# Two pairs of heads in step in a fused FNet and RWKV-7 block

## The chip, the cores and the metric

The program runs on one core of a Trainium2 chip. The metric is the device time of one execution, in microseconds (us), as the median over several runs. PE is TensorE, DVE VectorE, ACT ScalarE, POOL GpSimd; SP issues the DMAs of this kernel, all on one queue that is worked in order.

## The reference

```python
proj = x @ w_in                                   # 256 tokens, 2048 -> 512 + 3*1536 + 480 columns
y_fourier = real(fft2(proj[:512] in 4 groups))
p = p + (0.5*(prev + next) - p) * mu_shift        # centred shift of the other columns
r, k, v = ...                                     # 24 heads of 64, i.e. 12 pairs of heads
w_f, w_b = decay(tanh(low rank) @ w_up)           # low rank of 64, both directions
a_f, a_b = sigmoid(a0 + low rank @ a_up)
def step(state, r, w, k, v, a, b):                # along the tokens, forward and backward
    sa = state @ a
    state = state * w + outer(sa, b) + outer(v, k)
    return state, state @ r
y = group_norm(y_forward + y_backward); y = (y + bonus(r, k, r_k) * v) * (sigmoid(p_g) @ g_up)
h = layernorm(ALPHA*x + concat(y_fourier, y) @ w_out)
out = layernorm(ALPHA*h + (silu(h @ w_gate) * (h @ w_up)) @ w_down)     # 2048 -> 5632 -> 2048
```

All inputs are float32.

## The kernel before, in words

**Products.** A float32 weight tile is split in two: ACT casts it to float32r (`hi`), DVE subtracts that from the raw tile (`lo`), and the product is hi*hi + hi*lo + lo*hi. `weights()` loads one half tile of 512 KB into one of three `raw` buffers and splits it into two hi/lo pairs of 128x512, from rings of eight. A projection of 256 tokens onto 128 columns (`project`, `summed`) is 48 matmuls of 128x256 from two half tiles. Small products have plain float32 operands.

**The mixer** works on one pair of heads (128 columns) after the other, twelve in all. `prepare` computes K and R, the decays (low-rank products, exponentials), the normalised key and the scores `w` of each chunk of 64 tokens. The recurrence is chunked: four chunks a direction, and in each a 64x64 unit triangular matrix is inverted. `invert` does this in two parts. The 32x32 diagonal blocks are solved by substitution on POOL: 31 steps of two operations (`tmp` = product, `tt` = sum), on rows that DVE has laid out (`wt`, `wx`) and that DMAs take to DRAM (`md`) and back as a broadcast (`mt`). After the last step DVE transposes `tt` into `to`, and 32x32 matmuls on PE merge the blocks (`v1`, `xo`, into `ti`). `values` projects V into `sv`; `recur` walks the four chunks: `g` (scores times values) on PE, `gs` a copy by ACT, `u` = `ti` times `gs` on PE, copies into `sv`, `s` (the new state) on PE, and the outputs into the bank `yb`. A group norm (`bst`, `mv`, `rs`, `yn`) ends the pair, and its 128 rows go to DRAM as `mix`.

**The output projection** (`tokens_out` with `w_out`) takes `mix` back in, and runs over 32 half tiles of weights: four quarters of columns (q) by eight pairs of 128 rows, in an order by hand: of q 0 and 1 first the rows of `ORDER[:-1]`, then those of the last, then q 2 and 3. Its last `keep` tiles do their first 128 tokens before their other 128, so that the norm of the first half starts earlier; `keep` is half of the hi/lo pairs on hand (ring and `spare`). Then come the first norm, the gated feed-forward (176 half tiles) and the down projection (88, by `tokens_out` too, with eight further pairs as `spare`).

**What sets the order.** Nothing is issued as it is written. Operations are recorded with their dependences (`Program.add`), and `schedule` lists them with costs and latencies by hand, per engine; the best of 49 settings of two weights is issued. On PE it prefers, for a time, the array shape (rows by columns of the array that a matmul occupies) in use; `fused()` records several matmuls as one operation that nothing splits. Each engine works its list in order. Nearly all instructions carry the line of the loop that issues them (L307 before, L316 after), so rows are told apart by tile names.

Of the kernel before, what the change touches and what calls it, by code (L numbers as in the profile page):

```python
# [48 lines left out]
NV = V_LB + 12  # L49
# [18 lines left out]
class Program:  # L68
# [35 lines left out]
    def region(ap):  # L104

        dims, t = [list(d) for d in ap.ap], ap.tensor
        if "PSUM" in str(t._space):
            if not t.name.startswith("ch"):
                return 15, 15
            first = ap.offset % 512  # L110
            last = first + sum(s * (n - 1) for s, n in dims[1:])
            return 15, sum(1 << q for q in range(first // 128, last // 128 + 1))
        if "SB" not in str(t._space):
            return 1, 1
# [25 lines left out]
    def cost(self, eng, method, outs, ins, k, args):  # L140
# [3 lines left out]
        kw_op = k.get("op")  # L144
        if eng == "pe":
# [6 lines left out]
            return max(m, n) * 4 / 2.4 * side + 3 if m != 32 else 30  # L152
        if eng == "act":
            return 54 + 0.833 * n + 93 * ptrs + (40 if not psum else 0)
        if eng == "pool":
            if kw_op == OP.pow:
                return 500
            return (40 if method == "memset" else 147) + (0.9 if method == "memset" else 2.15) * n + 150 * ptrs
        if eng == "sp":
            return max(500, 4 * self.count(outs[0]) * list(outs[0].ap)[0][1] / 360)  # L160
# [3 lines left out]
        return 69 + (0.52 if half else 1.04) * n + 60 * ptrs  # L164
# [6 lines left out]
    def add(self, queue, method, args, kw):  # L171
# [27 lines left out]
        banks = {x.tensor.name for x in outs + ins if "PSUM" in str(getattr(x.tensor, "_space", ""))}  # L199
# [29 lines left out]
    def schedule(self, weight, hold):  # L229
# [14 lines left out]
        while left:  # L244
# [27 lines left out]
            if k is not None and k != kind[e]:  # L272
                kind[e] = k
                if e == 3:
                    t += 87
                    since = t
                else:
                    c += 1300
# [47 lines left out]
ORDER = (2, 3, 4, 5, 6, 0, 1, 7)  # L326
FOURIER = 0
# [4 lines left out]
def body(ctx, tc, i, out):  # L332
# [15 lines left out]
    ch.tiles = [t[:, c:c + 256] for c in (0, 256) for t in chain[2:]]  # L348
    nar = Ring(psum, "nar", [128, 512], 0)
    nar.tiles = [t[:, c:c + 128] for c in range(0, 512, 128) for t in chain[0:2]]  # L350
# [3 lines left out]
    def weights(src, spare=[]):  # L354
# [3 lines left out]
        for j in range(2):  # L358
# [3 lines left out]
            dve.tensor_tensor(lo, half, hi.bitcast(F32), op=OP.subtract)  # L362
# [26 lines left out]
    ws = Ring(consts, "w", [128, 2, 2, 4, 128], 3)  # L389
# [28 lines left out]
    hmu = consts.tile([128, 44], F32, name="hmu")  # L418
    omm = consts.tile([128, 44], F32, name="omm")
    dve.tensor_scalar(hmu, vec[:, V_MU:V_MU + 44], 0.5, None, op0=OP.mult)  # L420
    dve.tensor_scalar(omm, vec[:, V_MU:V_MU + 44], -1.0, 1.0, op0=OP.mult, op1=OP.add)
    hw0 = consts.tile([128, 48], F32, name="hw0")
    dve.tensor_scalar(hw0, vec[:, V_W0F:V_W0F + 48], 0.5, None, op0=OP.mult)
    hka = consts.tile([128, 12], F32, name="hka")
    omka = consts.tile([128, 12], F32, name="omka")
    dve.tensor_scalar(hka, vec[:, V_KA:V_KA + 12], 0.5, None, op0=OP.mult)
    dve.tensor_scalar(omka, vec[:, V_KA:V_KA + 12], -0.5, 1.0, op0=OP.mult, op1=OP.add)
    mhalf = consts.tile([128, 4], F32, name="mhalf")
    dve.memset(mhalf, -0.5)

    def project(wsrc, tl, src):
# [4 lines left out]
        for h in range(2):  # L436
            summed(acc, weights(wsrc[tl, h]), 8 * h, src)
# [6 lines left out]
    pps = ring("pp", [128, S + 2], 2)  # L444
    pss = ring("ps", [128, S], 1)
# [7 lines left out]
    def shifted(tl, dst):  # L453
        acc = project(i["w_in"], tl, xT)
        p, s = pps.next(), pss.next()
        act.activation(p[:, 1:S + 1], acc, AF.Copy, scale=hmu[:, tl:tl + 1])
        dve.tensor_tensor(s, p[:, 0:S], p[:, 2:S + 2], op=OP.add)
        dve.scalar_tensor_tensor(dst, acc, omm[:, tl:tl + 1], s, op0=OP.mult, op1=OP.add)


    lora = mx.tile([128, 2, S], F32, name="lora")
    low = mx.tile([128, 2, 2, S], F32R, name="low")
    for j, tl in enumerate((T_W, T_A)):
        t = lora[:, j, :]
# [3 lines left out]
        for d in range(2):  # L468
            (a0, a1), (b0, b1) = HEAD[d], HEAD[1 - d]
            act.copy(low[a0:a1, d, j, :], t[a0:a1])  # L470
            dve.tensor_tensor(low[b0:b1, d, j, :], t[a0:a1], low[a0:a1, d, j, :].bitcast(F32), op=OP.subtract)
    for j, tl in enumerate((T_G0, T_G1)):
# [9 lines left out]
    rmask = const("rmask", [128, 260])  # L482
    eye4 = const("eye4", [128, 8, 32])
    R = {n[0]: ring(*n) for n in (
        ("up", [128, 4, 128], 1), ("uh", [128, 4, 128], 1, F32R), ("ul", [128, 4, 128], 1, F32R),
        ("upg", [128, 2, 128], 1), ("k", [128, S], 1), ("th", [128, 2, S], 1), ("ta", [128, 2, S], 1),
        ("e", [128, 2, 4, 65], 1), ("f", [128, 2, 4, 65], 1), ("dec", [128, 4, 2], 3),
        ("kx", [128, S], 1), ("sq", [128, S], 1), ("kk", [128, S], 1), ("r", [128, S], 1),
        ("bs", [128, S], 2), ("xb", [128, 2, 4, 3, 64], 1), ("ar", [128, 2, 4, 3, 64], 3), ("bg", [128, 2 * S], 1),
        ("bk", [128, 2, 8, 64], 3), ("v", [128, S], 3), ("sv", [128, 4, 2, 2, 64], 2), ("wt", [128, 256], 1),  # L490
# [309 lines left out]
    for p in range(NPAIR):  # L800
        st = prepare(p)
        if p == FOURIER:
            fourier_in()
# [259 lines left out]
```

## Time and profile before

| | us |
|---|---|
| median of three runs (1424.67 to 1429.63) | 1426.9 |
| profiled execution, its own time | 1424.8 |
| its span, first to last instruction | 1422.9 |
| PE busy, share of the span | 1340.8, 94% |
| DVE, ACT, POOL busy | 954.1, 789.9, 501.5 |
| mean granted clock of TensorE | 0.974 of 2.4 GHz |

The mixer fills the first 610 us, the output projection lies across its end up to about 660 us, the feed-forward and the down projection fill the rest. Busy shares are means over these stages, so each stage has to be read by itself.

### The profile page before, as it was taken

Reading aid. Unit: us, or ns where it says so; the run is one execution under the profiler, and the core shown is the slowest. Engines: PE = TensorE matmul, PEld = TensorE weight load, DVE = VectorE, ACT = ScalarE, POOL = GpSimd, SP = SyncE. Lnnn points to the kernel's source line nnn. Section 1 sums busy time; section 2 is a strip of 40 time slices with the busy share of each in tenths; the row PEclk is TensorE's granted clock in tenths of the full one; section 3 lists DMA queues with packets and bytes.
Section 4 is the critical chain, followed back from the end, with each engine's and each line's share of the span. In section 5 each row is a group of like instructions: output and inputs, shape, how many; then the busy total and the mean of one; then the engine's idle time right before and its main releaser. Section 6 shows DMA issues by size and latency. Waiting matters only on the chain.

```text
span 1422.9 us, 26852 instructions
## 1 busy us (share of the span) xinstructions
PE 1340.8 (94%) x9828; PEld 1173.3 (82%) x9828; DVE 954.1 (67%) x1803; ACT 789.9 (56%) x1670; POOL 501.5 (35%) x1032
## 2 busy tenths in 40 slices
PE   8988999888889989998999999999999999999996
PEld 7987888878888876777888888888888888888886
DVE  6758778887888786668565556555555555555555
ACT  6556665666666665544555555555555554444441
POOL 1165878778888887102211111111111110000002
PEclk9999999999999998999999999999999999999998
DMA  8543332333333335463565555555555555656552
GB/s 277 189 152 119 105 112 94 109 103 103 116 116 101 105 125 175 156 202 127 195 237 181 192 187 185 191 186 185 191 184 188 192 181 195 194 195 195 194 196 102
DMA packets 73164, 232.32 MB, mean 163 GB/s; under 512 B 8136, under 2 KB 17224, under 8 KB 72392
## 3 DMA queue, kind: packets, MB, share of 16 engines
q1 hardware_dynamic: 73032, 230.61, 49.8%
q8 instruction: 77, 1.26, 0.4%
q14 instruction: 55, 0.45, 0.1%
HBM read 224.28 MB, written 6.29 MB: 162 GB/s over the span
## 4 chain that ended last, share of the span: by engine, by line
PE 63%; POOL 22%; DVE 7%; issue 4%; ACT 2%; DMA 1%; DVEq 0%; SPq 0%; POOLq 0%; ACTq 0%
PE ch L307 23%; PE mm L307 19%; PE sc L307 14%; POOL tmp L307 9%; POOL tt L307 9%; PE yb L307 7%; DVE lo L307 1%; POOL rs L307 1%; DVE w L307 1%; DVE f L307 1%; DVE ti L307 1%; ACT hi L307 1%; DVE yn L307 1%; POOL xb L307 1%; DMA mt<-md 1%
## 5 line engine op out<-in xcount | busy, mean ns | idle before, releaser
L307 DVE TENSOR_TENSOR lo<-raw,hi 128x512 fp32r<-128x512 f32 x758 | 555.5, 741 | 356.2 <-ACT hi L307 350.2
L307 ACT CAST hi<-raw 128x512 fp32r<-128x512 f32 x758 | 465.0, 620 | 411.0 <-PE mm L307 120.9
L307 PE MATMUL mm<-xT,hi 128*128 128x256 f32 (+1 forms) x1776 | 419.5, 320 | 6.7 <-ACT hi L307 5.6
L307 PEld LDWEIGHTS mm<-xT,hi 128*128 128x128 f32 x1776 | 301.8, 198 | 24.6 <-ACT hi L307 5.8
L307 PE MATMUL mm<-xT,lo 128*128 128x256 f32 (+1 forms) x1072 | 304.1, 292 | 0.0
L307 PEld LDWEIGHTS mm<-xT,lo 128*128 128x128 f32 x1072 | 209.9, 197 | 5.3 <-DVE lo L307 0.4
L307 PE MATMUL ch<-xT,hi 128*128 128x512 f32 x528 | 186.0, 399 | 0.0
L307 POOL TENSOR_TENSOR fe<-fe,fe 128x256 f32<-128x256 f32 x44 | 32.8, 747 | 406.0 <-DVE fe L307 385.6
L307 POOL TENSOR_TENSOR tmp<-mt,tt 128x60 f32<-128x60 f32 (+24 forms) x372 | 151.8, 408 | 52.5 <-DMA mt<-md 27.1
L307 POOL TENSOR_TENSOR tt<-tt,tmp 128x60 f32<-128x60 f32 (+24 forms) x372 | 141.8, 381 | 25.4
L307 PE MATMUL ch<-xT,lo 128*128 128x256 f32 x528 | 142.7, 281 | 0.0
L307 PE MATMUL sc<-xT,hi 128*128 128x512 f32 x352 | 121.9, 397 | 0.0
L307 PEld LDWEIGHTS ch<-xT,hi 128*128 128x128 f32 x528 | 97.2, 189 | 19.5
L307 PEld LDWEIGHTS ch<-xT,lo 128*128 128x128 f32 x528 | 99.8, 189 | 4.6
L307 POOL TENSOR_TENSOR lrs<-lrs,mhalf 128x1 f32<-128x1 f32 x4 | 3.9, 973 | 281.4 <-DVE lrs L307 281.4
L307 PE MATMUL sc<-xT,lo 128*128 128x256 f32 x352 | 93.3, 280 | 0.0
L307 PE MATMUL ch<-hi,h 128*128 128x512 f32 x264 | 88.4, 389 | 0.0
L307 PEld LDWEIGHTS sc<-xT,hi 128*128 128x128 f32 x352 | 63.8, 188 | 13.1
L307 PE MATMUL mm<-hi,h 128*128 128x512 f32 (+1 forms) x248 | 72.9, 358 | 0.0
L307 PEld LDWEIGHTS sc<-xT,lo 128*128 128x128 f32 x352 | 66.4, 189 | 2.9
L307 PE MATMUL yb<-xT,hi 128*128 128x512 f32 x176 | 63.7, 396 | 0.0
L307 PEld LDWEIGHTS ch<-hi,h 128*128 128x128 f32 x264 | 49.6, 188 | 10.4
(221 smaller groups left out, 2213.2 us busy)
## 6 DMA issues: line engine op xcount, KB each, us to landing
raw<-in_w_gu_dram SPq DMA_DIRECT2D x176, 512.0 KB, 3.8
raw<-in_w_down_dram SPq DMA_DIRECT2D x88, 512.0 KB, 4.2
raw<-in_w_in_dram SPq DMA_DIRECT2D x84, 512.0 KB, 3.5
raw<-in_w_out_dram SPq DMA_DIRECT2D x32, 512.0 KB, 3.6
mt<-md SPq DMA_DIRECT2D x12, 512.0 KB, 4.3
up<-in_lora_up_dram SPq DMA_DIRECT2D x12, 256.0 KB, 4.2
raw<-in_xT_dram SPq DMA_DIRECT2D x8, 256.0 KB, 4.7
raw<-in_w_in_dram SPq DMA_DIRECT2D x8, 256.0 KB
```

The lines of the kernel that those rows point to most:

```text
L307: getattr(o["q"].engine, method)(*args, **kw)
```

## The change

- **Two pairs in step.** The loop takes two pairs of heads at a time (`P`, six rounds), and the recurrence of round P-1 is written after the preparation of round P. `recur` does both pairs in each of its steps: one copy or state update serves both, each kind of product is one `fused` run of 64-row matmuls, and half-bank tiles of PSUM (`nar`) hold both pairs.
- **Substitution on 16x16 blocks.** `extract` computes the transposed score blocks on PE (eight 64x64 products a pair), masks them, and takes 16x4x16 pieces to DRAM, 16 DMAs a pair. `substitute` does 15 steps for both pairs at once, writes `tt` to DRAM (`ms`) and reads it back in 16 pieces as blocks of a 32x32 matrix (`eb`, and transposed `et`). `invert` merges 16 to 32 and 32 to 64 with 224 32x32 matmuls for two pairs, in runs that go round the four 32-row quadrants.
- **Low-rank products** are four plain float32 matmuls with 64 rows instead of eight in float32r, and the split of `up` into `uh`, `ul` goes.
- **Weights of the mixer:** POOL instead of DVE computes `lo` of the second half of each `w_in` tile (`shared`). The hi/lo rings have six buffers instead of eight.
- **Buffers:** `ch` has whole banks, `w`, `ar`, `bk`, `v` four buffers, `sv` and `ti` one for both pairs; `bonus` and gate products move to DVE.
- **Output projection:** `ORDER` and the order of tiles follow the pairs as they come ready; the Fourier projection moves from the first pair to the third. `spare` is empty, so `keep` is 3 instead of 5 here and 7 instead of 8 in the down projection.
- **Costs of the planner** are changed, among them those of POOL, of small DMAs, of partial partitions, and of a switch of the array shape.

```diff
-ORDER = (2, 3, 4, 5, 6, 0, 1, 7)
...
+ORDER = (2, 3, 4, 5, 0, 1, 6, 7)
...
     raws = Ring(consts, "raw", [128, 1024], 3)
-    his = Ring(consts, "hi", [128, 512], 8, F32R)
-    los = Ring(consts, "lo", [128, 512], 8, F32R)
+    his = Ring(consts, "hi", [128, 512], 6, F32R)
+    los = Ring(consts, "lo", [128, 512], 6, F32R)
...
-    def weights(src, spare=[]):
+    def weights(src, spare=[], shared=False):
...
-            dve.tensor_tensor(lo, half, hi.bitcast(F32), op=OP.subtract)
+            (pool if shared and j else dve).tensor_tensor(lo, half, hi.bitcast(F32), op=OP.subtract)
...
-            summed(acc, weights(wsrc[tl, h]), 8 * h, src)
+            summed(acc, weights(wsrc[tl, h], shared=True), 8 * h, src)
...
         th, ta = R["th"].next(), R["ta"].next()
...
-            js = slice(2 * d, 2 * d + 2)
-            dve.tensor_tensor(ul[a0:a1, js, :], up[a0:a1, js, :], uh[a0:a1, js, :].bitcast(F32), op=OP.subtract)
-        for d in range(2):
-            z = sc.next()
+        zs = sc.next(), sc.next()
+        with pr.fused():
             for j in range(2):
-                for u in (uh, ul):
-                    pe.matmul(z[:, j * S:(j + 1) * S], u[:, 2 * d + j, :], low[:, d, j, :], start=u is uh, stop=u is ul)
+                for d, (a0, a1) in enumerate(HEAD):
+                    pe.matmul(zs[d][:, j * S:(j + 1) * S], up[a0:a1, 2 * d + j, :], lora[a0:a1, 2 + j, :], start=True, stop=True)
+        for d, z in enumerate(zs):
...
+    def extract(p, st, mt):
...
+        tp, m0 = sc.next()[:, 0:S], R["sq"].next().rearrange("p (c s) -> p c s", s=64)
+        with pr.fused():
+            for c in range(4):
+                for h, (a0, a1) in enumerate(HEAD):
+                    pe.matmul(tp[a0:a1, c * 64:(c + 1) * 64], ar[a0:a1, 0, c, 0, :], xb[a0:a1, 0, c, 0, :], start=True, stop=True)
+        dve.tensor_tensor(m0, tp.rearrange("p (c s) -> p c s", s=64), tmask[:, None, :].to_broadcast([128, 4, 64]), op=OP.mult)
...
+            for d in (0, 1):
+                for n, (h, b, a) in enumerate(quads):
+                    for k in range(2):
+                        q, r, cs = n * 16 + k * 8 + 4 * d, slice(a + 16 * k, a + 16 * k + 16), slice(32 * b + 16 * k, 32 * b + 16 * k + 16)
+                        sp.dma_start(out=mdp[q:q + 4].rearrange("c (x y) -> x c y", y=16), in_=w[r, 1, h, :, cs] if d else m0[r, :, cs])
+            sp.dma_start(out=mt[:, p % 2].rearrange("p x y -> p (x y)"), in_=mdp[:, None].to_broadcast([64, 2, 256]))
...
+    def substitute(P, mt):
+        msp = ms[P % 2]
+        tt, tmp, e, et = (R[n].next() for n in ("tt", "tmp", "eb", "et"))
+        act.copy(tt, eye2[:, None].to_broadcast([128, 2, 8, 16]))
+        for s in range(15):
+            m, t = min(8, s + 1), 15 - s
+            x = tmp[:, 0:2 * m * t].rearrange("p (n j t) -> p n j t", n=2, t=t)
+            pool.tensor_tensor(x, mt[:, :, None, s + 1:16, s].to_broadcast([128, 2, m, t]),
+                               tt[:, :, 0:m, s:s + 1].to_broadcast([128, 2, m, t]), op=OP.mult)
+            pool.tensor_tensor(tt[:, :, 0:m, s + 1:16], tt[:, :, 0:m, s + 1:16], x, op=OP.add)
+        with pr.ahead(AHEAD):
+            sp.dma_start(out=msp.rearrange("(n p) x -> p n x", n=2), in_=tt.rearrange("p n m t -> p n (m t)"))
+            for j in range(2):
+                for n, (h, b, a) in enumerate(quads):
+                    for k in range(2):
+                        r = a + 16 * k
+                        sp.dma_start(out=e[r:r + 16, 8 * j:8 * j + 8, 16 * k:16 * k + 16],
+                                     in_=msp[j * 128 + r:j * 128 + r + 16].rearrange("(c u) (m t) -> (u m) c t", u=2, t=16))
+        dve.transpose(et.rearrange("p c t -> p (c t)"), e.rearrange("p c t -> p (c t)"))
+        return (e, et), (et, e)
...
+        with pr.fused():
+            for q in range(16):
+                j, d, c = q // 8, q // 4 % 2, q % 4
+                for h, b, a in quads:
+                    pe.matmul(vp[a:a + 32, q * 32:(q + 1) * 32], ws[j][a:a + 32, d, h, c, 32 * b:32 * b + 32],
+                              diag[d][1][a:a + 32, q, :], start=True, stop=True)
+        dve.copy_predicated(z.rearrange("p (n q) t -> p n (q t)", n=2),
+                            zmask.bitcast(mybir.dt.uint32)[:, None, :].to_broadcast([128, 2, 256]),
...
             u = nar.next()
-            for d in range(2):
-                pe.matmul(u[:, d * 64:d * 64 + 64], ti[:, d * 4 + cd[d], :], gs[:, d * 64:d * 64 + 64], start=True, stop=True)
+            with pr.fused():
+                for n, d, h, a0, a1 in jobs:
+                    o = n * 128 + d * 64
+                    pe.matmul(u[a0:a1, o:o + 64], ti[a0:a1, n * 8 + d * 4 + cd[d], :], gs[a0:a1, n, d, :], start=True, stop=True)
...
-    for p in range(NPAIR):
-        st = prepare(p)
-        if p == FOURIER:
-            fourier_in()
-        invert(p, st)
-        tokens(st)
-        values(p, st)
-        recur(p, st)
+    last = None
+    for P in range(NPAIR // 2 + 1):
+        if P < NPAIR // 2:
+            dec, mt = R["dec"].next(), R["mt"].next()
+            sts = []
+            for n in range(2):
+                sts.append(prepare(2 * P + n, dec[:, n]))
+                if P == 1 and n == 0:
+                    fourier_in()
+                extract(2 * P + n, sts[n], mt)
+                tokens(sts[n])
+                sts[n]["v"] = R["v"].next()
+                shifted(T_V + 2 * P + n, sts[n]["v"])
+            diag = substitute(P, mt)
+        if P:
+            recur(P - 1, *last)
+        if P < NPAIR // 2:
+            sv = R["sv"].next()
+            for n in range(2):
+                values(2 * P + n, sts[n], sv)
+            last = sts, invert(sts, diag), sv, dec
...
...
```

The order of POOL's instructions before, late in the mixer, within the substitution of one pair (`tmp`, `tt`); `bs` and `e` are of `prepare`:

```order
L307 TENSOR_TENSOR tmp_152<-mt_150,tt_151 128x54
L307 TENSOR_TENSOR bs_133<-th_121 128x256
L307 TENSOR_TENSOR tt_151<-tt_151,tmp_152 128x2x27
L307 MEMSET e_123 128x4 x2
L307 TENSOR_TENSOR tmp_152<-mt_150,tt_151 128x52
L307 TENSOR_TENSOR tt_151<-tt_151,tmp_152 128x2x26
```

The same engine after, in the last steps of the substitution of a round of two pairs:

```order
L316 TENSOR_TENSOR bs_124<-th_117 128x256
L316 TENSOR_TENSOR tmp_143<-mt_141,tt_142 128x48
L316 TENSOR_TENSOR lo_75<-raw_66,hi_69 128x512
L316 TENSOR_TENSOR tt_142<-tt_142,tmp_143 128x16x3
L316 TENSOR_TENSOR tmp_143<-mt_141,tt_142 128x32
L316 TENSOR_TENSOR tt_142<-tt_142,tmp_143 128x16x2
L316 TENSOR_TENSOR lo_77<-raw_67,hi_71 128x512
L316 TENSOR_TENSOR tmp_143<-mt_141,tt_142 128x16
L316 TENSOR_TENSOR lo_79<-raw_65,hi_73 128x512
```

One operation now serves two pairs, and the splitting of weights (`lo`) stands between the steps. On the SP queue, before, in the mixer (`raw` are the weights, `md` and `mt` the way through DRAM, `mix` a pair's result):

```order
L307 DMA raw_67<-in_w_in_dram 128x1024
L307 DMA md_182<-wx_148 128x256
L307 DMA raw_65<-in_w_in_dram 128x1024
L307 DMA raw_66<-in_w_in_dram 128x1024
L307 DMA mt_150<-md_182 128x1x1024
L307 DMA mix_174<-ym_164 128x256
```

And after, in the steady part of the mixer (`ms` is the store after the substitution, `eb` its pieces):

```order
L316 DMA md_173<-w_90 16x4x16 x8
L316 DMA raw_65<-in_w_in_dram 128x1024
L316 DMA md_173<-sq_122 16x4x16 x8
L316 DMA ms_175<-tt_142 128x2x128
L316 DMA upg_115<-in_lora_up_dram 128x256
L316 DMA raw_66<-in_w_in_dram 128x1024
L316 DMA eb_144<-ms_175 16x8x16 x16
L316 DMA mt_141<-md_173 128x1x256
L316 DMA mix_163<-yn_150 128x256
L316 DMA mix_164<-yn_150 128x256
L316 DMA raw_67<-in_w_in_dram 128x1024
```

Each `md` and `eb` row is 8 or 16 DMAs, between loads of weights. On PE, before, at the first merge of a pair (`mm` is a projection, `ch` with `to` or `t` a merge):

```order
L307 MATMUL mm_84<-xT,hi_70 128x256
L307 MATMUL ch_89<-to_149,w_94 32x32 x4
L307 MATMUL ch_89<-t_155,w_94 32x32 x4
L307 MATMUL ch_89<-to_149,w_94 32x32 x4
L307 MATMUL ch_89<-t_155,w_94 32x32 x4
L307 MATMUL mm_84<-xT,hi_70 128x256
```

And after, in the merges of a round of two pairs (`sc` is the scores' product in `extract`):

```order
L316 MATMUL ch_86<-eb_144,z_146 32x32 x16
L316 MATMUL ch_86<-et_145,z_146 32x32 x16
L316 MATMUL ch_86<-eb_144,z_146 32x32 x16
L316 MATMUL ch_86<-et_145,z_146 32x32 x16
L316 MATMUL sc_83<-xb_126,ar_128 64x64 x8
L316 MATMUL mm_80<-xT,lo_77 128x256
```

Runs of four became runs of 64 and more, of which successive matmuls lie in different quadrants of the array. Up to the last merge PE changes 496 times between projections and other matmuls before, and 317 times after; over the whole program it changes the array shape 299 times before and 290 after. The program's matmuls are 8402 before and 9506 after, instructions on POOL 1037 and 545, on SP 513 and 798.

## Rows read from the trace of the kernel before

**Rows 1.** The page: busy time of each engine, and its 40 slices.
```profile
PE 1340.8 (94%) x9828; PEld 1173.3 (82%) x9828; DVE 954.1 (67%) x1803; ACT 789.9 (56%) x1670; POOL 501.5 (35%) x1032
...
POOL 1165878778888887102211111111111110000002
PEclk9999999999999998999999999999999999999998
```
**Rows 2.** Windows: stretch, length; busy of PE, PEld, DVE, ACT, POOL; clock; DMA.
```profile
207.00:458.00 251.00, 225.17 (x2466) 202.39 (x2466) 208.66 (x488) 163.42 (x405) 206.07 (x457) 0.95 0.33 105
612.00:656.00 44.00, 43.53 (x216) 36.47 (x215) 27.90 (x48) 16.45 (x29) 0.00 (x0) 1.00 0.58 187
656.00:680.00 24.00, 17.80 (x131) 16.28 (x130) 21.92 (x38) 12.38 (x22) 14.45 (x10) 0.95 0.29 88
700.00:900.00 200.00, 200.00 (x1139) 174.09 (x1138) 120.31 (x182) 112.58 (x221) 29.36 (x38) 1.00 0.60 198
```
**Rows 3.** The chain of waits from 292 to 334 us, by line.
```profile
by line: POOL tmp L307 28.5%; POOL tt L307 28.0%; issue 10.2%; DVE ul L307 3.9%; POOL nt L307 3.3%; DVE f L307 3.1%; POOL xb L307 2.7%; DVE ti L307 2.7%; DVE yn L307 2.6%; POOL rs L307 2.5%; POOL dec L307 1.9%; POOL bs L307 1.6%; DVE v1s L3
```
**Rows 4.** Single tiles: count, ns least/median/most, first and last start in us.
```profile
L307 DVE STREAM_TRANSPOSE to<-tt x12: 429/445/447, 115.6 to 572.1; 128x256 f32<-128x256 f32 x12
...
L307 DVE TENSOR_SCALAR yn<-yb,mv,rs x48: 301/335/346, 164.6 to 608.3; 128x64 f32<-128x64 f32 x48
```
**Rows 5.** The same windows view, `tmp` and `tt` apart: POOL's part in it.
```profile
207.00:458.00 251.00, 148.18 (x372) 0.95 0.33 105
```
**Rows 6.** Instruction groups of POOL and DVE: busy us, mean ns of one, idle before.
```profile
L307 POOL TENSOR_TENSOR th<-th,k 128x512 f32<-128x512 f32 x12 | 17.7, 1473 | 39.6 <-DVE nt L307 38.9 <-DVE th L307 0.7
...
L307 POOL TENSOR_TENSOR xb<-th,e 128x512 f32<-128x512 f32 x12 | 15.2, 1269 | 0.1
...
L307 POOL TENSOR_TENSOR tmp<-mt,tt 128x60 f32<-128x60 f32 x36 | 14.9, 413 | 2.7
...
L307 POOL TENSOR_TENSOR bs<-th 128x256 f32<-128x256 f32 x12 | 11.0, 918 | 0.0
...
L307 DVE TENSOR_TENSOR lo<-raw,hi 128x512 fp32r<-128x512 f32 x758 | 555.5, 741 | 356.2 <-ACT hi L307 350.2 <-PE mm L307 2.2 <-PE ch L307 1.1
```
**Rows 7.** Timeline of PE in the mixer: start us, length us, group, matmuls in it.
```profile
335.64 0.21 PE L307 MATMUL ch<-to,w 32*32 32x32 f32 x1
335.73 0.19 PE L307 MATMUL ch<-t,w 32*32 32x32 f32 x1
...
343.30 0.89 PE L307 MATMUL ch<-ti,v1s 32*32 32x32 f32 x32
...
357.32 0.45 PE L307 MATMUL ch<-sv,w 128*64 128x64 f32 x8
...
358.39 0.55 PE L307 MATMUL ch<-gs,ti 128*128 128x64 f32 x4
...
359.31 0.40 PE L307 MATMUL mm<-xT,hi 128*128 128x256 f32 x2
...
359.67 0.40 PE L307 MATMUL mm<-xT,hi 128*128 128x256 f32 x2
```
**Rows 8.** The chain of waits from 612 to 656 us: start, length, what.
```profile
620.50 19.05 PE ch L307 x84
```
**Rows 9.** DMA issues: KB of one, us to landing; SP's time for one.
```profile
raw<-in_w_in_dram SPq DMA_DIRECT2D x84, 512.0 KB, 3.5
...
mt<-md SPq DMA_DIRECT2D x12, 512.0 KB, 4.3
...
md<-wx SPq DMA_DIRECT2D x12, 128.0 KB, 2.1
...
L307 SPq DMA_DIRECT2D md<-wx x12: 326/327/425, 71.4 to 525.2; - x12
```
**Rows 10.** What the SP queue waited for: us in total, times, longest us.
```profile
SPq L307 <- DVE lo L307: 703.6, 261, 12.2
...
SPq L307 <- DVE w L307: 26.0, 5, 17.3
```

More of the change, by code (lines that the diff above doesn't have):

```diff
@@ L678, in invert @@
-        for h, (a0, a1) in enumerate(HEAD):
-            act.copy(w[a0:a1, :, h, :, 0:64], ar[a0:a1, :, :, 0, :])
-        st["ti"] = ti
-    def recur(p, st):
-        w, ar, bk, sv, ti, dec = (st[n] for n in ("w", "ar", "bk", "sv", "ti", "dec"))
-        y = ybank.next()
+        with pr.fused():
+            for n in range(8):
+                for h, d, s, t, cs in jobs:
+                    pe.matmul(v1[t:t + 32, n * 32:(n + 1) * 32], ws[n // 4][s:s + 32, d, h, n % 4, cs:cs + 32], t1[s:s + 32, n, :],
+                              start=True, stop=True)
@@ L726, in recur @@
-            for h in range(2):
-                for d in range(2):
-                    o0, cb = 64 * (cd[d] % 2), (cd[d] // 2) * 128 + h * 64
-                    pe.matmul(y[o0:o0 + 64, cb:cb + 64], w[:, d, h, cd[d], 64:128], sv[:, cd[d], d, h, :],
-                              start=first and h == 0, stop=c == 3 and h == 1)
-        bp, gp, bg, up = ch.next(), ch.next(), R["bg"].next(), R["upg"].next()
-        sp.dma_start(out=up, in_=i["lora_up"][p, :, 4:6])
-        pe.matmul(bp, ones2, st["bs"], start=True, stop=True)
@@ new lines, in recur @@
+            with pr.fused():
+                for n, h, d in order:
+                    pe.matmul(yv(n, h, d, cd[d]), sts[n]["w"][:, d, h, cd[d], 64:128], sv[:, n, cd[d], d, h, :],
+                              start=first and n == h == 0, stop=c == 3 and n == h == 1)
+            if c < 3:
+                f = dec[:, :, c + 1, :, None]
+                s = s.rearrange("p (n d i) -> p n d i", n=2, i=64)
+                if not first:
+                    dve.tensor_tensor(sd, s, state, op=OP.add)
+                    s = sd
+                for h, (a0, a1) in enumerate(HEAD):
+                    dve.tensor_tensor(rows(sv, nx, h, (a0, a1)), s[a0:a1], f[a0:a1].to_broadcast([64, 2, 2, 64]), op=OP.mult)
+                if c < 2:
+                    (dve if first else pool).tensor_tensor(state, s, f.to_broadcast([128, 2, 2, 64]), op=OP.mult)
@@ new lines, in recur @@
+        for n in range(2):
+            pool.tensor_tensor(ym[:, n, :], ym[:, n, :], sts[n]["v"], op=OP.add)
+        gp = ch.next()
+        for n in range(2):
+            up = R["upg"].next()
+            sp.dma_start(out=up, in_=i["lora_up"][2 * P + n, :, 4:6])
+            with pr.fused():
+                for j in range(2):
+                    pe.matmul(gp[:, n * S:(n + 1) * S], up[:, j, :], lora[:, j, :], start=j == 0, stop=j == 1)
+        dve.tensor_tensor(ym.rearrange("p n s -> p (n s)"), ym.rearrange("p n s -> p (n s)"), gp, op=OP.mult)
@@ L761, in body @@
+        for n in range(2):
+            sp.dma_start(out=mix[4 + 2 * P + n], in_=ym[:, n, :])
     fin = [dram.tile([128, S], F32, name=f"fin{g}") for g in range(4)]
```

352 lines of the change are left out of this document (169 added, 183 removed), and 4 rows, old and new, of the table R.

## The prediction, on record before the changed kernel ran

> **What bounds the kernel now.** I read the page first. PE is busy 94% of the span, POOL 35% [rows 1], but that is a mean over stages: the slices show POOL near or above 80% in the mixer and almost idle behind it. So I went on by windows. From 700 to 900 us PE is busy 200 of 200 us at clock 1.00, and ACT and DVE have 112.6 and 120.3 [rows 2]: the feed-forward is PE's alone, and only fewer matmuls could shorten it. The output projection between 612 and 656 is nearly as full (43.53 of 44); in the 24 us behind it PE has 17.80, where the first norm shows [rows 2].
>
> The mixer is different. The transpose `to`, once a pair, starts first at 115.6 and last at 572.1 us [rows 4]: eleven intervals of 41.5 us. The window from 207 to 458 us holds six pairs, 41.8 us each, and in one pair PE is busy 37.5, DVE 34.8, POOL 34.3 and ACT 27.2 us, at a clock of 0.95 [rows 2]. PE therefore idles 4.3 us a pair and loses some more by the clock. The chain of waits from 292 to 334 us, one period, says why: 28.5% is `tmp` and 28.0% `tt`, the substitution, and further POOL operations stand in it [rows 3]. That is one dependent series of 62 operations, 148.18 us for six pairs, 24.7 a pair [rows 5], 0.4 each, and POOL's other work (34.3 - 24.7 = 9.6) stands in the same list. POOL with the waits around it sets the period; PE is close behind.
>
> **The change, part by part** (per pair, unless said otherwise).
>
> *POOL.* The substitution becomes 30 operations for two pairs, of 16 to 128 elements a partition. No row has just these shapes; `tmp` with 60 elements takes 0.413 and `bs` with 256 takes 0.918 [rows 6]. Bounds: 30 x 0.413 = 12.4 and 30 x 0.918 = 27.5 for two pairs, 6.2 to 13.8 a pair. I take 0.47, since most have 60 to 128 elements or fewer: 7. New on POOL are six `lo` operations of 128x512. POOL operations of that size take 1.27 and 1.47 [rows 6]; I take 1.37, so 8.2. Sum: 9.6 + 7 + 8.2 = 24.8, at the upper ends 9.6 + 13.8 + 8.8 = 32.2. Either way POOL falls below PE's 37.5 and stops being the bound by its sum.
>
> *DVE and ACT.* DVE loses the six `lo` at 0.741 [rows 6], 4.4, and the layout of the rows, and gains the bonus and gate products, one predicated copy and masks: under 31 from 34.8. ACT loses the split of `up`. Neither limits; nothing is credited.
>
> *PE.* In `recur`, a step's `u` for a pair took 0.55 in one row of 128-row products, while eight records of 64-row products take 0.45 [rows 7]: 0.10 x 4 steps is 0.4, and by the pitch to the next rows up to 0.65; I take 0.5 off. The merges grow from 64 to 224 calls for two pairs. A row of 32 records, two a call, in a single quadrant took 0.89, so 56 ns a call; two quadrants in alternation show rows of 0.2 that start 0.09 apart [rows 7], so they overlap. Bounds: 56 ns a call (no overlap), 6.3 a pair, and a quarter of it, 14 ns (four beside each other), 1.6; now it is 1.8. I take 25 ns, being nearer to the overlapping rows: 2.8, +1.0. The eight products of `extract` are worth 0.3 to 0.45 by the same 64-row rows; the low-rank products, half as many at a slower type, come out even. Net +0.5 to +1.0; I take +0.5 with the shorter tails (bounds -0.8 to +4.8).
>
> The Trainium skill, "TensorE: Matmul & The Clock Gate", Part 3, the section on packing small matmuls by row and column tiling, has matmuls on different tiles of the array run concurrently; by it the merges would be at the quarter, 3.1 us for two pairs, and the mixer 1.25 x 11 = 14 us shorter than I sum. The overlapping rows agree in direction; four at once is shown by none.
>
> *The period.* With POOL out of the way PE's idle 4.3 shrinks to about 0.5. The clock was 0.95 while PE was idle every so often, and 1.00 where it was full [rows 2]; of 37.5 x 0.05 = 1.9 I give back half, since runs alternate with small work still (317 times instead of 496). 37.5 + 0.5 - 0.95 + 0.45 = 37.5, against 41.8: -4.3. Eleven periods: -47.
>
> *Fill and drain.* The first round must prepare two pairs before its substitution starts, and the last round's recurrence is for two pairs. From the last `to` to the last `yn` it is 36.2 us now [rows 4]. Beside it lie 14 half tiles of `w_out`: in both versions those of q 0 and 1 that do not need the last two pairs' rows, each 12 matmuls of 0.227 [rows 8], 38 us together. That cover hides a drain of the present length; a longer one costs. I take 0 (bounds -10 to +15).
>
> *Output and down projection.* `keep` falls from 5 to 3: two tiles less of matmuls for the second half of the tokens cover the first norm, 2 x 6 x 0.227 = 2.7 [rows 8]; the norm's window has 6.2 us of PE idle now [rows 2], so I charge all 2.7 (0 if the covered part was long enough). In the down projection one tile less, 0 to 1.4; I take 0.3.
>
> *Rings of six.* In the feed-forward PE is busy 200 of 200 while ACT and DVE stand at 56 and 60% [rows 2]; two buffers less cost 0 as long as the loads arrive in time. A half tile lands in 3.5 us [rows 9] and is used in 24 x 0.12 = 2.9 (three records of a projection in 0.36 [rows 7]); three raw buffers cover that. If they did not, every half tile of the 264 behind the mixer would show it.
>
> *SP.* 48 tiny DMAs for two pairs in `md`/`eb`, and three more, at 0.327 each [rows 9]: 17 us of issue in 75. It is no bound by its sum. What queues behind them is weights; see the rivals.
>
> Sum against the profiled execution's own 1424.8: -47 + 2.7 + 0.3 + 0 = 1381. That execution is 2.1 us (0.15%) under the median of the runs, so I give **1382**.
>
> **The rivals.**
>
> *A, central: PE bounds the mixer, 36 to 39 us a pair.* For it: rows 2 and 3. That is -64 to -31 in place of -47: 1366 to 1399, with the unknown ends 1362 to 1402. Chance 0.50.
>
> *B: PE packs well.* Runs are no longer broken up, and the clock stays at 1.00 as in the output projection. Then 37.5 x 0.95 = 35.6, +0.5, less the tails: a small run's row lasts 0.17 longer than its pitch, and there are (496 - 317) / 12 = 15 changes, 7.5 runs, fewer a pair, 1.3. That is 34.8, -7.0 x 11 = -77: 1353, range 1340 to 1362. Against it: the mixer's PE work is still full of small waits. Chance 0.17.
>
> *C: the loop of dependences binds.* `sv`, `ti`, `mt` and the half banks are single; a round's way from scores through `md`, `mt`, 30 operations, `ms`, `eb`, merges and recurrence is long: 42 (one period's preparation) + 8.5 + 4.3 (landing of `mt` [rows 9]) + 15 to 30 + 8.5 + 36 = 114 to 129 us for two rounds in flight, 57 to 65 a round against the 75 of A. It binds only above 150, so not by the mean; with queueing in lists worked in order it may come near, at 39 to 41.5 a pair: 1402 to 1422. Chance 0.14.
>
> *D, the other side: the SP queue stalls the weights.* The queue is in order, and the planner puts `md`, `ms` and `eb` first whenever they are ready. A round has three points where the queue stands: for the scores, for the end of the substitution, and for the landing of `ms` ahead of `eb`. Already now SP waits up to 17.3 us for `w` [rows 10]. Eight or sixteen issues of 0.327 plus the 2.1 of a landing come to about 5 to 8.5 us a stall. Three raw and six hi/lo buffers hold at most some 2.9 x 3 = 8.6 us of projection work. It decides from the point where a stall outlasts that: 4 us over, three times a round, is +6 a pair against A's 37.5, a period of 43.5, +19 instead of -47: 1448; range 1432 to 1475. For it: the waits of rows 10, and that the cover now is eight buffers. Against it: the order has weights between the groups. Chance 0.14.
>
> The 64-byte runs of `md` bear on D. The Trainium skill, "DMA: Bandwidth & Descriptors", section Specifications, says that writes under 512 B become a read-modify-write; by it the landings of the tiny DMAs would be longer than the 2.1 us I use and D likelier. No run so far shows such small runs landing.
>
> *E: nothing moves,* since PE's 37.5 swells by the merges at 56 ns (+4.5) and eats the 4.3: 1422 to 1431. Chance 0.05.
>
> **The numbers.** The likeliest is A, 1382. The range leaves out D, the upper part of E and the very bottom of B, not quite 2 in 10 together: 1342 to 1424. Faster by over 0.3%, about what a measurement of this kernel can tell from no change, are A, B and C: 0.81; within it E, 0.05; slower D, 0.14. Within A alone the range is 1362 to 1402.
>
> **What would show it.** In the changed trace the distance of two `et` transposes should be about 75 us, the busy share of POOL in the mixer near two thirds, its chain of waits mostly PE; the merges' rows should come to about 25 ns a call; the clock in the mixer 0.97 or more; `lo` on POOL 1.3 to 1.5 each and seldom the releaser of PE. B shows as PE over 97% busy in the mixer, C as a chain through `md`, `ms`, `eb` and the recurrence with PE idle, D as SP waits above 8 us ahead of `raw` and PE released by `hi` or `lo`. Idle of PE around the first norm should grow by up to 2.7 us. The prediction is wrong if PE is busy less than 90% of the mixer, if the drain after the last `et` exceeds 45 us, or if the feed-forward no longer runs at 200 of 200.

## The result

The changed kernel takes 1440.5 us (median of four runs, 1439.3 to 1441.3), the kernel before 1427.7 beside it: a ratio of 1.0091, interval 1.0071 to 1.0111. It is slower by 0.9%, where 1382 was predicted and nothing above 1424 lay in the range.

The page of the changed kernel, in the parts shown of before [rows 1] (busy time of each engine; the 40 slices):

```profile
PE 1344.1 (93%) x12132; PEld 1172.2 (81%) x12132; DVE 852.4 (59%) x1427; ACT 704.3 (49%) x1367; POOL 398.2 (28%) x540
...
POOL 3548437484744714002211111111111110000002
PEclk9999899899999989999999999999999999999999
```

POOL, DVE and ACT all have less to do, PE as much as before. The windows view (steady mixer, drain, output projection with the norm, a piece of the feed-forward):

```profile
166.00:569.30 403.30, 357.88 (x5824) 316.99 (x5824) 251.97 (x493) 190.44 (x409) 217.57 (x319) 0.94 0.35 109
569.30:622.00 52.70, 45.84 (x847) 34.40 (x847) 27.21 (x63) 21.65 (x43) 5.07 (x6) 0.97 0.50 167
622.00:672.00 50.00, 46.26 (x223) 39.28 (x224) 28.68 (x45) 19.26 (x32) 0.00 (x0) 0.93 0.52 169
672.00:700.00 28.00, 23.77 (x148) 21.38 (x147) 24.78 (x44) 13.70 (x24) 14.05 (x10) 0.82 0.27 85
700.00:900.00 200.00, 200.00 (x1140) 174.12 (x1139) 116.74 (x179) 110.78 (x216) 27.84 (x36) 1.00 0.59 198
```

The stages are cut at single instructions (tile view: count, ns, first and last start): `et`, once a round, answers to `to` [rows 4]; then the last `mix`, then the first silu:

```profile
L316 DVE STREAM_TRANSPOSE et<-eb x6: 693/711/714, 166.0 to 569.3; 128x512 f32<-128x512 f32 x6
...
L316 SPq DMA_DIRECT2D mix<-yn x12: 327/424/1089, 236.2 to 621.9; - x12
...
L316 ACT ACTIVATE fe<-fe x44: 401/415/419, 715.0 to 1184.9; 128x256 f32<-128x256 f32 x44
```

From these and the same points of other traces (for before the second `to`, at 168.4 us, is the start of ten pairs; "to silu" is last `mix` to first silu):

| profiled execution, us | fill | ten pairs | drain to last mix | to silu | rest |
|---|---|---|---|---|---|
| before | 168.4 | 403.7 | 39.8 | 88.1 | 723.0 |
| changed | 166.0 | 403.3 | 52.6 | 93.1 | 724.4 |
| before, short substitution (e1) | 160.7 | 395.9 | 39.8 | 86.4 | 723.0 |
| before, with small DMAs (e12) | 184.9 | 432.4 | 41.2 | 86.8 | 723.0 |
| changed, no small DMAs (e4) | 153.8 | 376.9 | 55.6 | 92.9 | 724.6 |
| changed, long runs (e5) | 158.8 | 382.4 | 57.6 | 93.2 | 724.4 |
| changed, second gate buffer (e6) | 164.9 | 389.3 | 52.7 | 95.0 | 724.5 |
| changed, planned with SP's price (e17) | 165.4 | 382.0 | 55.6 | 92.3 | 724.4 |

The ten pairs take what they took. PE idles 45.4 us in them (403.3 - 357.9), before 41.4, at a clock of 0.94 in both. The 16.4 us that the changed profile is longer are the drain (+12.8), the stretch behind it (+5.0) and the end (+1.4), less 2.4 in the fill.

What PE waits for in the ten pairs of the changed kernel (waits view: us in total, times, longest; "issue" is idle time that ends with nothing that it waited for):

```profile
PE ch L316 <- issue: 15.5, 8, 3.5
PE ch L316 <- DVE et L316: 7.3, 3, 4.1
PE ch L316 <- DVE yn L316: 3.4, 4, 1.0
PE ch L316 <- DMA upg<-in_lora_up_dram: 3.4, 3, 1.3
...
PE mm L316 <- DVE lo L316: 0.2, 1, 0.2
```

A third of PE's 45.4 idle us are stops without a wait in runs of small matmuls; before there is no such entry. Split weights (`lo`) are named for 0.2 us only. Weights and `mt` come late elsewhere, at the casts of ACT and the substitution on POOL (in the ten pairs of before: never at the casts, 1.2 us for `mt`):

```profile
ACT hi L316 <- DMA raw<-in_w_in_dram: 18.9, 12, 6.4
...
POOL tmp L316 <- DMA mt<-md: 15.4, 4, 6.5
```

SP's list shows what such loads stand behind. The timeline of SP (start, length, what; a row groups issues):

```profile
404.20 0.37 SPq L316 DMA_DIRECT2D raw<-in_w_in_dram  x1
404.68 0.38 SPq L316 DMA_DIRECT2D ms<-tt  x1
405.28 0.52 SPq L316 DMA_DIRECT2D mt<-md  x1
405.85 0.58 SPq L316 DMA_DIRECT2D raw<-in_w_in_dram  x1
408.12 7.42 SPq L316 DMA_DIRECT2D eb<-ms  x16
415.64 1.31 SPq L316 DMA_DIRECT2D raw<-in_w_in_dram  x3
```

Sixteen `eb` issues hold SP for 7.4 us, and right behind them three `raw` are issued in a row, 0.44 us each: their buffers had been free and waiting. The waits of SP (us in total, times, longest), where `w` had 26.0 in five before [rows 10]:

```profile
SPq L316 <- DVE w L316: 73.7, 17, 14.2
```

### The profile page after: what moved, and what is told of

Read it like the earlier page. It is cut to its first block, busy times and chain, and to the rows that moved or that the text cites. A ratio compares the mean times of both kernels' runs of the same rounds, so it can differ in the third digit from the quotient of the medians.

```text
span 1439.5 us, 30790 instructions
## 1 busy us (share of the span) xinstructions
PE 1344.1 (93%) x12132; PEld 1172.2 (81%) x12132; DVE 852.4 (59%) x1427; ACT 704.3 (49%) x1367; POOL 398.2 (28%) x540
## 4 chain that ended last, share of the span: by engine, by line
PE 51%; DVE 0%; DVEq 0%; issue 0%
PE ch L316 19%; PE mm L316 14%; PE sc L316 12%; PE yb L316 6%; DVE w L316 0%; DVE lrs L316 0%; DVEq L1122 0%; DVE lst L316 0%; DVE lmv L316 0%
## 5 line engine op out<-in xcount | busy, mean ns | idle before, releaser
L316 DVE TENSOR_TENSOR lo<-raw,hi 128x512 fp32r<-128x512 f32 x676 | 495.3, 737 | 382.7 <-ACT hi L316 358.5
L316 PE MATMUL mm<-xT,hi 128*128 128x256 f32 (+1 forms) x1776 | 414.4, 320 | 13.3 <-ACT hi L316 6.4
L316 POOL TENSOR_TENSOR lo<-raw,hi 128x512 fp32r<-128x512 f32 x84 | 115.0, 1372 | 143.9 <-ACT hi L316 106.9
L316 POOL TENSOR_TENSOR tmp<-mt,tt 128x96 f32<-128x96 f32 (+13 forms) x90 | 49.2, 547 | 19.2 <-DMA mt<-md 15.4
```

Of the source, the lines that this page charges most:

```text
L316: getattr(o["q"].engine, method)(*args, **kw)
```

## The experiments

Times are medians, beside runs of the kernel before on the same chip (1426 to 1428); ratios are to it. "Order kept" means that the planner's order was computed for the unchanged program and operations were left out or replaced only when it was issued, so that nothing else moves.

**e1, e2: a shorter substitution.**
```diff
+            pr.skip = s >= 16      # e1, kernel before, 31 steps; e2, changed kernel: s >= 5 of 15
```


> The kernel before, its instruction order kept, with the last 15 of the 31 steps of the substitution left out (30 POOL operations a pair, about 11 us of the 24.7; the blocks are not fully inverted). If POOL's series sets the period of the mixer before, as the prediction had it, the period falls from 41.5 to about 37.5, where PE's 37.2 busy us stop it, and the time to 1375 to 1390. If PE's own list in order (its work, its lower clock and many short waits) sets it, the time stays at 1415 or more.

1409.3, ratio 0.9876 (0.9848 to 0.9904). Between the two: 11 us a pair off POOL make the period 39.6 for 40.4, and PE's idle 3.6 a pair for 4.1. The ten pairs in the windows view:

```profile
160.70:556.60 395.90, 360.07 (x3915) 318.13 (x3915) 325.82 (x776) 259.49 (x659) 222.28 (x446) 0.94 0.37 118
```

So POOL's series was a bound before, but with this order PE's list stood about 1 us a pair behind it, not 4.

> The changed kernel, order kept, with the last 10 of the 15 steps left out (20 POOL operations for two pairs, about 10 us; the blocks are not fully inverted). If the way through the substitution (scores, md, mt, the steps, ms, eb, merges) closes the loop that sets the round of 80.7 us, up to 10 us a round come off: 1385 to 1410. If PE's list sets it, only the waits for et shrink, at most 2 us a round: 1428 to 1440.

1440.8, ratio 1.0097 (1.0066 to 1.0128): no change against 1.0091. It does not clear the way through the substitution, though. The last step here ended at 294.1 us, and SP issued `ms` only at 320.3, behind two groups of `md` that waited for scores (SP's timeline):

```profile
290.45 14.67 SPq L318 DMA_DIRECT2D raw<-in_w_in_dram  x3
311.44 4.54 SPq L318 DMA_DIRECT2D md<-w  x8
316.08 0.37 SPq L318 DMA_DIRECT2D raw<-in_w_in_dram  x1
316.55 3.66 SPq L318 DMA_DIRECT2D md<-sq  x8
320.26 0.43 SPq L318 DMA_DIRECT2D ms<-tt  x1
```

With the order kept, what POOL gained was lost in SP's list.

**e3, e13: the stalls inside the merges.** PE's timeline of the changed kernel, in a run of 32x32 matmuls, shows a stall with nothing that it waits for (in brackets the idle time and its releaser). The 15.5 us of such stalls are those of the ten pairs, five rounds; over all six rounds they are 19.2, so the 15.5 that the expectation gives for six is that of five.

```profile
429.49 0.40 PE L316 MATMUL ch<-eb,z 32*32 32x32 f32 x25 [3.51 <-issue]
```

```diff
-            for q in range(16):
-                for h, b, a in quads:
+            for h, b, a in quads:
+                for q in range(16):
```


> The changed kernel, same order of operations, with the 32x32 matmuls of each merge run going through one quadrant after the other, not round the four. In the trace of the change PE stands still for 1.9 to 3.5 us in the middle of such runs with nothing to wait for, 15.5 us over six rounds. If it is the pace of the small matmuls that outruns the supply of instructions, at 56 ns a call in place of 26 the stalls go, the runs take about 6 us a round longer, and the time stays within 1436 to 1465. If the stall belongs to the number of instructions and not to their pace, it stays too, and the time is 1465 to 1485.

1505.5, ratio 1.0565 (1.0516 to 1.0615), outside both ranges. The stalls are gone, but a record (one of the two that a float32 call leaves in the trace) takes about 42 ns on the mean in place of about 13, some 75 us more over 2688 records. One quadrant takes 28 ns a record at full clock (0.89 us for 32 [rows 7], clock 1.00 there) and 52.6 at 0.50 (next run), and the clock over the ten pairs is 0.84 here; so the forecast's 56 ns a call was too short.

> Nothing of the block is computed: PE does 768 32x32 matmuls round the four quadrants with all else quiet, 384 quadrant by quadrant, and 768 round the four while 24 half tiles of weights are loaded. If the stalls in the merges are the supply of instructions, the first run shows gaps of 2 us and more without a wait once some hundred calls are through, the second, at over 50 ns a call, none, and the third as many or longer ones. If they come from the data or the banks of the merges, none of the three has a gap.

Nothing of the block is computed here. Round the four quadrants PE stops after 223 records and then after every 128 (with their weight loads 256 instructions), as the expectation of a supply limit had it. The 24 loads, meant for the third run, were all issued within the first 40 us, beside the first run. The third run in PE's timeline:

```profile
103.32 1.93 PE L354 MATMUL bank<-z 32*32 32x32 f32 x128 [1.42 <-issue]
106.78 1.92 PE L354 MATMUL bank<-z 32*32 32x32 f32 x128 [1.53 <-issue]
110.78 1.93 PE L354 MATMUL bank<-z 32*32 32x32 f32 x128 [2.08 <-issue]
```

From start to start of the records the stops are 1.7 to 2.3 us there, and 2.0 to 4.8 in the first run while the loads ran. Quadrant by quadrant, at 52.6 ns a record and clock 0.50, there is none.

The trace of the changed kernel itself agrees. In three rounds there are two stops of over 1 us (at 342.70 and 346.15, 511.51 and 516.61, 577.17 and 582.27 us), and each time the trace has exactly 256 matmuls and weight loads from the first to the second. The one at 516.61 stands before a product of the scores, not of the merges, so it is the count of instructions that decides and not the data of the merges.

**e4, e5, e12: the small DMAs.**
```diff
 e4:  the md pieces and the eb pieces are not issued
 e5:  out=mdp[...] as 2 or 4 rows of 1 to 2 KB, in_=w or m0 likewise; eb from rows of a constant
 e12: (kernel before) 24 pieces of w, 16x4x16, to a DRAM tile, right after the store md
```


> The changed kernel without the 16 small DMAs a pair into md and the 16 a round into eb (the merges then work on zeros and on other data; mt and ms are still moved). Order otherwise nearly the same. If the SP queue and the small pieces set the round (rival D), 4 us or more a pair come off: below 1400. If they only make the waits for et (12 us in all) and the late start of mt, 5 to 20 us come off: 1420 to 1435.

1410.4, ratio 0.9880 (0.9847 to 0.9913): 30 us under the changed kernel, between the two cases. The ten pairs, windows view, and PE's waits in them:

```profile
153.80:530.60 376.80, 342.91 (x5820) 305.19 (x5819) 251.43 (x494) 189.20 (x408) 217.58 (x319) 0.96 0.35 112
```

```profile
PE ch L318 <- issue: 10.8, 8, 3.2
...
PE ch L318 <- DVE et L318: 2.0, 1, 2.0
```

37.7 us a pair, with 3.4 idle. Of the 26.5 us that the ten pairs lose, 11.5 are idle time of PE, the stops and the wait for `et` above all, and 15.0 its busy time, at a clock of 0.96 for 0.94. The fill loses 12.2 more.

> The changed kernel, order kept, each of the 288 small DMAs replaced by one of the same place, size class and, for md, the same wait, but with runs of 1 to 2 KB in place of 64 B (the merges work on other data; the eb loads no longer wait for ms). If it is the 64-byte runs that cost (slow landings, or packets in the way of the weights), the time falls as without the pieces, to 1405 to 1420. If it is the issue and the waits on the SP queue, it stays at 1430 to 1442.

1423.1, ratio 0.9978 (0.9957 to 0.9998): 17 us come back, between the two. SP's time for one issue is shorter (tile view of `md`, changed kernel, then e5; ns least/median/most):

```profile
L316 SPq DMA_DIRECT2D md<-w x96: 303/424/1251, 67.5 to 522.2; - x96
```

```profile
L316 SPq DMA_DIRECT2D md<-w x96: 223/252/315, 65.1 to 500.1; - x96
```

The sum over all 288 is 133 us of SP in the changed kernel (22 a round), 82 in e5, none in e4; the profiles are 1439.5, 1416.5 and 1403.7 us long. In e5 the `eb` loads also no longer wait for `ms`, and the runs that are moved are fewer; this experiment doesn't separate the three.

> The kernel before, order kept, with 24 more small DMAs a pair (16x4x16 pieces of the scores into a DRAM tile that nothing reads) behind the store md on the SP queue: as many as the change has. If their issue on SP is what ate the gain, the weights and mt come later by about 24 x 0.45 = 11 us of SP a pair, and the time rises by 20 us or more: above 1446. If the pieces are harmless in a mixer with one small load a pair, it stays below 1436.

1469.6, ratio 1.0291 (1.0272 to 1.0309). POOL's waits, kernel with pieces:

```profile
POOL tmp L307 <- DMA mt<-md: 71.2, 10, 34.9
```

Before it was 27.1 in two over the whole program. SP issues pieces for 130 us, the waits for `mt` grow by 44 us in sum, and the time rises by 42. Here too PE waits for no weights in the ten pairs.

**e7, e10, e15, e16: other queues.** The pieces (order kept), or the `w_in` loads (with the second gate buffer of e6, planned anew), issued by ACT or POOL.
```diff
+        pr.alt = nc.scalar      # e7; nc.gpsimd: e10; e15 and e16 the same for the w_in loads
```


> The changed kernel, order kept, with the 288 small DMAs issued by ACT in place of SP, at the same places of the order. If the pieces cost because they stand ahead of weights and mt on the SP queue, 10 to 25 us come off (ACT is busy less than half of the mixer): 1415 to 1430. If they cost by the way they land, or if ACT is held up as SP was, 1435 to 1460.

> The changed kernel, order kept, with the 288 small DMAs issued by POOL in place of SP. Without them on SP the steady rounds took 75.4 us in place of 80.7 and the fill 12 us less; POOL is busy 54% of the mixer. If POOL issues one in about 0.5 us and its own work has the room, most of it comes back: 1412 to 1430. If POOL pays more for each than SP, or its substitution and its lo wait behind the pieces as ACT's casts did, 1440 to 1480.

> The changed kernel with the second buffer for the gate weights, and the 84 loads of w_in tiles issued by ACT in place of SP, so that the small DMAs stand ahead of no weights. If the weights behind the pieces are what PE lacks, and ACT (47% busy) can issue 14 loads a round at 0.33 to 0.45 us, the time falls below the kernel before: 1405 to 1422. If ACT, which waits for each free buffer in its own order, holds up its casts and copies, 1430 to 1470.

> The same with POOL issuing the w_in loads, at 0.51 us each (7 us a round of an engine that is busy 54%). If POOL's list leaves the loads room, 1408 to 1425; if they stand behind the steps of the substitution and the lo operations there, as the pieces stood ahead of them on POOL before, 1435 to 1480.

1461.9 (ratio 1.0248), 1480.0 (1.0386), 1437.4 (1.0081), 1451.2 (1.0160): each of them the slower case (e7 1.9 us above its range). ACT takes 0.41 to 0.44 us to issue a piece, POOL 0.51, and each has its own work behind it. With the weights on ACT (e15), PE's wait for `et` is 16.6 us in five (7.3 in three in the changed kernel, 11.7 in five in e6), and the ten pairs take 387.5 for the 389.3 of e6: the pieces' own way is late even where no weights share their queue, and clearing the queue of weights brought next to nothing there.

**e6, e9: a second buffer for the gate weights.**
```diff
-            up = R["upg"].next()
+            up = bg[:, 1, :].rearrange("p (a b) -> p a b", a=2) if n else R["upg"].next()
```


> The changed kernel with a second buffer (a spare half of bg) for the gate weights of the second pair, so that their load need not wait for the first pair's product. At the end of the mixer that wait stood ahead of the last mix and of a PE gap of 4.8 us, with the clock at 0.57 behind it. If this is what the drain lost, 3.5 us of the gap and about as much by the clock come back: 1432 to 1437. If the drain is the two pairs' recurrence itself, nothing: 1438 to 1442.

> As the run with a second buffer for the gate weights, but with the instruction order of the changed kernel kept on every engine. If the 10 us came from the SP queue, which no longer stands until the first pair's product is done before it issues that load (and the weights behind it), they come again: 1428 to 1433. If they came from the other order that the planner picked, the time is 1434 to 1441, with the gap of 4.8 us at the end of the mixer smaller.

1430.0 (ratio 1.0038, 1.0015 to 1.0060), under both cases, and 1437.0 (1.0091, 1.0060 to 1.0123). The second ratio is that of the changed kernel, so with the order kept no gain is clear of the noise; the gap of 4.8 at the end stays at 4.76, because PE's list has the product at a fixed place. What e6 gained is thus mostly the planner's new order. My first reason, the drain, was wrong: it is 52.7 in e6.

**e8, e14, e17, e18: the planner.**
```diff
-    pr.flush(TRIES)
+    pr.flush([(100, 250)])                      # e8
-        with pr.ahead(AHEAD):
+        with pr.ahead(0):                           # e14, for md, mt, ms, eb; with e6's buffer
-            return max(330 if size < 16384 else 500, ...)
+            return max(460 if size < 16384 else 500, ...)   # e17; e18 also 27 for 15 a 32x32
```


> The changed kernel with the planner held to another of its 49 settings (100, 250) for the mixer: the same operations in another order. If the order that the planner happens to pick is worth as much as the parts of the change, the time moves by more than 10 us; if not, it stays within 8 us of 1440.

> The changed kernel with the second buffer for the gate weights, planned anew, and without the priority that puts md, mt, ms and eb ahead of the weights on the SP queue. If it was that priority that made the weights late, 10 us or more come off the 1430 of that kernel: 1410 to 1422, faster than before. If the pieces' issue time itself costs, wherever it stands, the time is 1425 to 1440.

> The changed kernel with the second buffer for the gate weights, planned with 460 ns in place of 330 for a small DMA on SP, as the trace has it. The pieces' issue time stays; the order of the weights and of ms around them is planned with it. If a better order can hide the pieces, the time falls below the kernel before: 1410 to 1424. If the time that the queue needs is the cost, whatever the order, it stays at 1427 to 1437, like 1430 and 1434 of the two other plans.

> The same with 27 ns in place of 15 for a 32x32 matmul besides (13 a record were measured, two records a call). Either way as the run before; a spread of 5 us or more between the two would be the planner's own, since what they compute is the same.

1444.3, 1433.9, 1424.2 (ratio 0.9974, 0.9954 to 0.9995) and 1434.7. The priority was not it. e17 is the one complete kernel at or below the kernel before, at the edge of what can be told; e18 computes the same and is 10 us slower. e6, e9, e14, e17 and e18 are one set of operations in five orders: 1424 to 1437.

**e11: fewer tiles held back, alone.** `keep = 3` in the kernel before.

> The kernel before with three in place of five last tiles of the output projection held back for the second half of the tokens, the rest as it was. The stretch from the last mix to the first silu was 88.1 us before and 93.1 after; 4.8 of it at its start are a wait for mix with a lower clock behind it, the rest the norm. If keep costs what its two tiles cover, 2 to 3.5 us are lost: 1428 to 1431. If the cover was long enough, 1425 to 1427.5.

1426.1, ratio 1.0007 (0.9993 to 1.0021): nothing.

## Why the prediction was wrong

*What held.* POOL's sum fell as worked out: 21.8 us a pair in the ten pairs (predicted 24.8), of it 7.4 for the substitution (7), and 1.372 a `lo` (1.37). A 32x32 call took about 26 ns inside its runs, stops apart (25). PE's busy time fell a little, 35.8 a pair for 36.2. The feed-forward stayed at 200 of 200.

*The step that failed* is "with POOL out of the way PE's idle 4.3 shrinks to about 0.5". It is 4.5 a pair in the changed kernel, and still 3.6 and 3.4 in e1 and e4. Three things stood in its place. Of the 60 us by which the sum missed the profile, 44 lie in the fill and the ten pairs (2.8 came off, not 47), 13 in the drain and 3 behind it.

First, the SP queue, which was rival D with 0.14, and which the sum had dismissed as "no bound by its sum". The price was too low (0.327, from the row of `md<-wx` [rows 9]; the pieces took 0.42 in the median and 0.46 on the mean), but 22 us in a round of 80 are no bound by their sum either. The place was not counted: SP works in order, `mt`, `ms`, `eb` and the weights wait behind pieces that wait for scores or for `ms`, and the timeline above shows it. That the pieces cost is shown by e4 (-30 without them) and e12 (+42 when added to the kernel before). D had it through the weights alone. Of its signs, SP waits above 8 us came (14.2 for `w`), but PE released by `hi` or `lo` did not: PE names weights for 0.2 us in the ten pairs, and the pieces' own way into `mt` and `et` is late (e2, e12, e15). D's cover was also counted too small: three raw buffers and three half tiles in the rings are six half tiles, 17 us at its 2.9, not 8.6. The weights are late at ACT's casts (18.9 us), and ACT and POOL work their lists in order, so they may act on PE that way; how the 30 divide between the two ways is not settled.

The Trainium skill, "DMA: Bandwidth & Descriptors", section Specifications, has transfers under 512 B become a read-modify-write, which led me to expect slow landings. No run here shows those as the cost: `md` pieces landed in 1.5 to 2.2 us, and what the short runs lengthened was SP's issue.

Second, the merges, which the sum had priced by their pace alone (+1.0 a pair). Their stops had no row before: 15.5 us in the ten pairs, 1.6 of the 4.5 idle us a pair, one to two a round of up to 3.5 us. e13 and the spacing of 256 in the changed kernel show what they are: the supply of instructions. With them a pair's merges come to about 4.5 us (112 calls of 26 ns and 1.6) for the predicted 2.8. Their size is read from the trace; e3, which removed them, paid more for it. In e4 they fell to 10.8, so the pieces may lengthen them; no run separates that.

Third, POOL was worth less. The chain of waits [rows 3] gave POOL more than half of the period, but a chain names what ended last, not how far behind the next one is. e1 took 130 us of POOL's work out and 17 came off. Where the pieces are gone as well (e4), the period is 37.7, the 37.5 of the sum; but with PE busy 34.3 and idle 3.4, where the sum had 37 and 0.5, so it is right in size and not in its parts. Even there fill and ten pairs are 41.4 us shorter than before (-47 in the sum), and the drain and the stretch behind it take 20.6 of them back. The base was high too: 41.8 is the mean of six pairs, ten take 40.4, and the first of the eleven intervals is 52.9 us of the fill.

*The drain* was charged 0 with +15 as its bound, and cost 12.8, and 5.0 behind it. From the last `to` or `et` to the last write of `ti` it is 17.3 us (before 10.3), the recurrence 21.4 (19.1), from there to the last `mix` 13.8 (10.4): the merges of two pairs, with two stalls, make most of it. The 14 tiles of `w_out` ran out at 620.9, and PE stood (timeline):

```profile
625.74 0.80 PE L316 MATMUL mm<-hi,xT 128*128 128x512 f32 x1 [4.80 <-ACT xT L316]
```

From 624 to 632 us, the end of that gap and what follows, the clock was 0.57, and the norm at 672 to 700 us ran at 0.82 where it had 0.95 [rows 2]. No experiment undid this; its size is read from the trace only.

*The norm*: `keep` was charged 2.7 and costs nothing in the kernel before (e11).

*A slip in the working*: by the sum's own terms C's 39 to 41.5 us a pair give 1399 to 1427, not 1402 to 1422.

*Not run*: the planner's new costs, the rings of six and `lo` on POOL, each alone in the kernel before. What they add to or take from the 403.3 us is open.

## What to carry to other kernels

Before a bound is relieved, measure the distance to the next one: leave part of its work out with the order kept, as e1 does, and see what comes off. Then read in the changed trace what the engine itself names as its waits: here the late weights of the rival were hardly among them, and the stops that no row of before could show were the largest. Count the issues of a queue that works in order by their measured time and by what stands behind each one's wait; many small DMAs can cost more than the operations that they save. Where a list scheduler decides the order, changes of one per cent lie within the spread of its plans (13 us here for the same operations), so a part of a change is judged with the order kept.

## What the runs showed of the hardware

Sustained runs of 32x32 matmuls round four quadrants are held by the supply of instructions (e13): 128 records take 1.7 us and are followed by a stop of 1.8 us, with loads in flight up to 4.8. That is 27 ns a record at a clock of 0.50, where one quadrant takes 52.6, and about what one quadrant takes at full clock (28 ns [rows 7]). The 223 records before the first stop, at clock 1.00, came at the same 13.4 ns as the 13.3 of the later ones at 0.50. The Trainium skill, "Runtime: NRT & Kernel Launch", section Instruction fetch mechanics, says that instructions are refilled in blocks of 256 and that the cost of crossing into the next block is mostly hidden; the block agrees with the trace, the hiding doesn't at this pace. The issue of one small DMA takes SP 0.42 us with 64-byte runs and 0.25 to 0.29 with runs of 1 to 2 KB (e5); with 64-byte runs ACT takes 0.41 to 0.44 (e7) and POOL 0.51 (e10).
